# An earlier softplus for the later attention heads, a sigmoid by exponential and reciprocal, pinned splits, and decode logits by wide products and a sum

## The chip, the cores and the metric

The kernel runs on one core of a Trainium2 chip, in one launch. The metric is the device time of that launch in microseconds. A core has five engines with a queue of their own each: TensorE (PE: matrix products into PSUM, with its weight loads as PEld), VectorE (DVE), ScalarE (ACT: activation functions and casts), GpSimd (POOL) and SyncE (SP: here it only issues DMAs). An engine runs its instructions strictly in the order in which the program was laid down for it, and waits on semaphores for the others.

## The reference

One step of one layer of a decoder: 16 meta rows and 512 prompt rows go through causally, and beside them eight sequences with four new rows each read a paged cache of 512 past positions (four pages of 128). Width 2048, eight heads of 128, all in float32. Cut to what matters here:

```python
h = rmsnorm(x, g_pre)
q, k, v, ga, cb, cc, ch, gc, ma, mc = jnp.split(h @ w_in, split_offsets(), axis=-1)
a = attend(q, k, v, b_sb) * jax.nn.silu(ga)                        # 8 heads
c = cb * causal_conv(cc * ch, w_conv, b_conv) * jax.nn.silu(gc)    # width 3
merged = (jax.nn.sigmoid(ma + b_gate[:D_MODEL]) * (a @ w_pa)
          + jax.nn.sigmoid(mc + b_gate[D_MODEL:]) * (c @ w_pc))
y = x + rmsnorm(merged @ w_out, g_post)

def stick_breaking(q, k, v, q_pos, k_pos, b_sb):
    z = einsum('bqhd,bkhd->bhqk', q, k) * HEAD_DIM ** -0.5 + b_sb
    mask = k_pos[None, :] < q_pos[:, None]
    log_keep = where(mask, log_sigmoid(-z), 0.0)
    after = cumsum(log_keep, axis=3, reverse=True) - log_keep
    attn = where(mask, exp(log_sigmoid(z) + after), 0.0)
    return einsum('bhqk,bkhd->bqhd', attn, v)
```

Attention has no softmax. Each score z gives a softplus, the softplus values of the later keys are summed, and the weight is the exponential of score minus sum.

## The kernel before, in words

Every matrix product is made to float32 accuracy from three products of a cheaper kind: each operand is split into a high part (a cast on ScalarE, `act.copy`) and a low part (a subtraction on VectorE), and PE multiplies high by high, high by low and low by high. `w_split` (line 237) does this for 128 x 1024 pieces of weights, in three buffers; `split_evac` (492) for everything else. Activations lie transposed, features on the partitions and the 528 + 32 rows (560) on the free axis.

The stages follow each other on PE:

1. *Start*: load and normalise x, first products.
2. *Projections of the heads* (`head_now` 693 for heads 0 to 3, which are also attended at once; `head_later` 709 for heads 4 to 7, whose k, v and q go to DRAM scratch).
3. *Column pairs* (`pair` 987 over `seven` 949, PE's products at line 946): two times 128 columns of w_in by seven instead of eight half products. Each pair is one group of work of about 21 us, and 36 such groups follow one another: silu gates of the heads (1 to 4), the convolution (5 to 20), and the sigmoid gates MA and MC (21 to 36, the loop at 1089). The last pair of the loop is `j == 14`, `w == 1`: two blocks of columns, two halves each, so four sigmoid operations.
4. *The stage of w_pc* (1159): for each of 16 column blocks `j`, `gemm` with c (PE's line 256). Among them stand the four later heads, `HERE = {0: 4, 2: 5, 5: 6, 8: 7}`: `attend` for the head, then `gated`.
5. *The stage of w_pa* (1191), which needs all heads (a_hl), then *w_out*, then the rows' norm and the stores.

*Decode attention* is spread over stages 2 and 3 by a generator, `decode_steps` (734), which `dec_step` advances. A step of its first part is one cache page: 128 positions by four heads are multiplied with the four new rows' queries and summed over 128 elements, sixteen `tensor_tensor_reduce` operations at line 756, each with one column of `z_all` as its sum. There are 64 such pages (two halves of the heads, eight sequences, four pages). Then come decode's softplus, its sums and exponentials, and its products with the value pages (line 831), whose pool `dec3` is closed right before the pool `split0` of head 4's split parts is opened in the same place. `dec_group` (875) says how many steps each group of stage 3 takes: up to group 25 none, 2, 2, 2, then one each up to 20 and four each after that, as long as there are logits; from 26 on one each, but two at 26 and 28.

*A later head's chain* (`attend`, 599): the scores z (PE, line 610) of three groups of tiles, B, C and A; for each group softplus in four ScalarE operations (Abs, Exp, Ln, Relu: `softplus_acts`, 466), pinned to follow one another; sums and splits on VectorE and ScalarE; PE adds the sums to z (line 679); an Exp (683), a mask and a split per group; PE multiplies with v (line 689). `gated` multiplies with the silu gate (1136) and splits into `a_hl`. The next head's k, v and q are loaded (`head_loads`, 715, on SP's queue) and split (`head_split`, 1108) behind the w_pc block after the head's own, line 1174. Head 4 is loaded during the last gates and split at 1112.

What sets the order of the work: the program is laid out by a planner that goes through the traced instructions, keeps data dependences and buffers, and places each instruction on its engine when its time model says that it can begin, so an engine's order need not be the program's. `pin` (line 144, `tc.keep_in_program_order`) forbids this: a pinned instruction stays behind all that was traced before it on its engine. Before, the softplus operations of later heads and the loads of ScalarE's tables (`preload_act_table_set`) are pinned, the splits and the exponentials of attention aren't. The table that holds Exp, Ln and Abs (`LNEXP`) is loaded at 1095, after the last pair's sigmoids. `c_hl` lies in the room of `h_hi` (tag "A") and `a_hl` in that of `h_lo` (tag "B"). The c values are loaded and split at 1128 to 1132, in four buffers that the gates' loads of this stage use too.

Of the kernel before, what the change touches and what calls it, by code (L numbers as in the profile page):

```python
# [17 lines left out]
P = 128  # L18
# [42 lines left out]
def hybrid_step_kernel(  # L61
# [430 lines left out]
    def split_evac(hi, lo, raw_hi, raw_lo, scale=None):  # L492
        if scale is None:
            act.copy(hi, raw_hi)
# [53 lines left out]
    def k_split(pl, kr):  # L548
        khi = pl.tile([P, T], F32R, name="khi")
        klo = pl.tile([P, T], F32R, name="klo")  # L550
        split_evac(khi, klo, kr, kr)
        return khi, klo

    def v_split(pl, vn):
        vhi = pl.tile([P, 5, P], F32R, name="vhi", bufs=1)
        vlo = pl.tile([P, 5, P], F32R, name="vlo", bufs=1)
        split_evac(vhi[:, 0:4, :], vlo[:, 0:4, :], vn[:, 0:4, :], vn[:, 0:4, :])
        split_evac(vhi[0:16, 4, :], vlo[0:16, 4, :], vn[0:16, 4, :], vn[0:16, 4, :])
        return vhi, vlo
# [33 lines left out]
    def q_split(pl, qr):  # L593
        qhi = pl.tile([P, T], F32R, name="qhi")
        qlo = pl.tile([P, T], F32R, name="qlo")
        split_evac(qhi[:, NMETA:TP], qlo[:, NMETA:TP], qr, qr)
        return qhi, qlo

    def attend(pl, h, khi, klo, vhi, vlo, qhi, qlo, pl_a=None, after=None):
# [71 lines left out]
        for g in GROUPS:  # L671
            zt = gt[g]
            for st, c0, n, ts, m in tiles_of(g):
                ops = [(zt[:m, c0:c0 + n], neg_u[:m, :m], x) for x in sp_[st]]
                if st < 4:
                    m2, n2 = sf_[st + 1][0].shape
                    ops += [(zt[:m, c0 + n - n2:c0 + n], neg_one[:m2, :m], x) for x in sf_[st + 1]]
                for i, (o, l, x) in enumerate(ops):
                    pe.matmul(o, lhsT=l, rhs=x, start=False, stop=(i == len(ops) - 1), skip_group_check=True)  # L679
        for g in GROUPS:  # L680
            zt = gt[g]
            A = tl("e", g)
            act.activation(A, zt, AF.Exp, bias=b)
# [50 lines left out]
    def decode_steps():  # L734
# [3 lines left out]
        for said, part in (("part", units[:DEC1]), ("logits", units[DEC1:])):  # L738
            with tc.tile_pool(name="dec1", bufs=2, side="right") as d1:
                for hf, b in part:  # L740
# [8 lines left out]
                    for pg in range(NPG):  # L749
                        kt = d1.tile([P, 512], F32, name="kpage", bufs=3)  # L750
                        first(page_load(kt, kc, b, pg, cs))
                        for i, qt in enumerate(qts):
                            for t in range(2):
                                for h in range(4):
                                    junk = d1.tile([P, P], F32, name="junk", bufs=2)
                                    dve.tensor_tensor_reduce(  # L756
                                        out=junk, in0=kt[:, h * P:(h + 1) * P], in1=qt[:, t, h * P:(h + 1) * P],
                                        scale=1.0, scalar=0.0, op0=ALU.mult, op1=ALU.add,
                                        accum_out=z_all[:, pg, b, 4 * hf + h, 2 * i + t:2 * i + t + 1])
# [328 lines left out]

    for j in range(0, KD, 2):
        for w, c in ((0, COL_MA), (1, COL_MC)):  # L1090
            gs = [q_tile("g") for _ in range(2)]
            for m, half, b in pair(c + j * P, HQ):
                act.activation(gs[m][:, by_query(m, half)], b, AF.Sigmoid, bias=gate_bias(j + m, w))
            if j + 2 * w == KD:
                tc.keep_in_program_order(act.preload_act_table_set(LNEXP))
# [12 lines left out]
    def head_split(pl, x):  # L1108
        kr, vn, qr = x
        return *k_split(pl, kr), *v_split(pl, vn), *q_split(pl, qr)  # L1110

    parts = head_split(hs0, loaded)
# [10 lines left out]
    cp2 = cctx.enter_context(tc.tile_pool(name="later2", bufs=1))  # L1123
# [336 lines left out]
```

## Time and profile before

| | |
|---|---|
| median of 3 runs | 1590.72 us (1590.13 to 1592.11) |
| profiled execution | 1588.02 us |
| its span | 1586.4 us |
| mean granted clock of TensorE | 0.992 |
| ScalarE busy | 761.2 us, 48% of the span |
| GpSimd busy | 236.8 us, 15% of the span |
| weights' high parts, line 240, ScalarE | 259.4 + 132.0 us |
| weights' low parts, line 241, VectorE | 301.2 + 154.0 us |
| logits, line 756, VectorE | 1024 operations, 244.6 us by the groups' table |
| chain that ended last | 95% PE, 2% VectorE, 1% ScalarE |

The span runs from the first to the last instruction; the execution's own time is 1.6 us longer. A busy share is an average over stages with different limits, so the table of stretches, which gives each engine's busy time in a chosen part of the span, says more than the totals. The chain that ended last goes back from the last instruction: at each step to what released it, or to the instruction before it on its engine. In the list of waits a line reads: engine, what waited, what it waited for, then the total in us, how many times, and the longest. A pair of numbers in front of an instruction is its start and its length in us.

### The profile page before, as it was taken

How to read it: one execution, taken by the hardware profiler on the slowest of the kernel's cores; microseconds unless marked ns; L12 is line 12 of the kernel's file. 1: busy time of each engine (PE TensorE's matmuls, PEld its weight loads, DVE VectorE, ACT ScalarE, POOL GpSimd, SP SyncE). 2: the span in 40 equal slices, each digit the busy share in tenths (PEclk: the TensorE clock that was granted, in tenths of full speed). 3: DMA queues.
4: the chain of work that ended last, by engine and by line, in shares of the span. 5: the costliest groups of instructions: out<-in, count | busy, mean ns of one | idle time of the engine just before them, and what ended most of it. 6: DMA issues, size and time to landing. Idle time of an engine off the chain costs nothing.

```text
span 1586.4 us, 32330 instructions
## 1 busy us (share of the span) xinstructions
PE 1563.9 (99%) x12172; PEld 1528.4 (96%) x12172; DVE 1268.2 (80%) x3574; ACT 761.2 (48%) x1345; POOL 236.8 (15%) x428
## 2 busy tenths in 40 slices
PE   8999999999999999999999999999999999999997
PEld 8999999999999999999999998889899989999997
DVE  7329999956899999999999997566677667877776
ACT  6245555435444444444444467444465543355562
POOL 1133333222111011010011102321100000000000
PEclk9999999999999999999999999999999989999999
DMA  8246556344554444345456545856595525433345
GB/s 262 82 141 180 160 170 183 108 128 136 171 161 147 138 141 145 123 145 158 119 181 176 174 142 162 274 172 203 182 322 172 168 88 178 152 103 98 101 137 189
DMA packets 300675, 252.77 MB, mean 159 GB/s; under 512 B 11522, under 2 KB 268614, under 8 KB 299702
## 3 DMA queue, kind: packets, MB, share of 16 engines
q1 hardware_dynamic: 272021, 160.45, 35.1%
q0 software_dynamic: 28368, 89.98, 16.9%
q8 instruction: 95, 1.56, 0.4%
q14 instruction: 63, 0.51, 0.1%
q10 hardware_dynamic: 128, 0.27, 0.1%
HBM read 217.95 MB, written 32.71 MB: 158 GB/s over the span
## 4 chain that ended last, share of the span: by engine, by line
PE 95%; DVE 2%; ACT 1%; issue 1%; DMA 1%; DVEq 0%; ACTq 0%; SPq 0%
PE mm L946 33%; PE mm L256 27%; PE o L946 24%; PE mm L321 2%; PE z L679 1%; PE o L689 1%; PE z L321 1%; PE tp L831 1%; PE z L610 1%; PE z L1401 1%; PE tp L505 0%; PE z L1255 0%; DMA raw<-in_w_in 0%; DVE wlo L241 0%; PE tp L158 0%
## 5 line engine op out<-in xcount | busy, mean ns | idle before, releaser
L240 ACT CAST whi<-raw 128x1024 fp32r<-128x1024 f32 x247 | 259.4, 1051 | 362.2 <-PE mm L946 131.4
L241 DVE TENSOR_TENSOR wlo<-raw,whi 128x1024 fp32r<-128x1024 f32 x247 | 301.2, 1220 | 89.1 <-ACT whi L240 87.7
L946 PE MATMUL mm<-h_hi,whi 128*128 128x272 f32 (+1 forms) x1152 | 333.5, 290 | 0.7 <-ACT whi L240 0.7
L946 PE MATMUL mm<-h_hi,wlo 128*128 128x272 f32 (+1 forms) x1152 | 332.6, 290 | 0.0
L946 PE MATMUL mm<-h_lo,whi 128*128 128x272 f32 (+1 forms) x1152 | 332.5, 289 | 0.0
L946 PE MATMUL o<-t_hi,whi 128*128 128x272 f32 (+1 forms) x864 | 250.2, 290 | 1.5 <-DVE c L972 1.5
L946 PE MATMUL o<-t_lo,whi 128*128 128x272 f32 (+1 forms) x864 | 249.8, 289 | 0.0
L946 PE MATMUL o<-t_hi,wlo 128*128 128x272 f32 (+1 forms) x864 | 249.6, 289 | 0.0
L756 DVE CUSTOM_DVE_ANT_0 junk<-kpage,qb 128x128 f32<-128x128 f32 x1024 | 244.6, 284 | 4.0 <-DMA qb<-q_scr 3.6
L946 PEld LDWEIGHTS mm<-h_hi,whi 128*128 128x128 f32 x1152 | 217.3, 189 | 6.1 <-ACT whi L240 3.5
L946 PEld LDWEIGHTS mm<-h_lo,whi 128*128 128x128 f32 x1152 | 216.8, 188 | 0.9 <-issue 0.8
L946 PEld LDWEIGHTS mm<-h_hi,wlo 128*128 128x128 f32 x1152 | 216.9, 189 | 0.2
L240 ACT CAST whi<-s 128x1024 fp32r<-128x1024 f32 x126 | 132.0, 1048 | 154.6 <-PE mm L946 50.6
L241 DVE TENSOR_TENSOR wlo<-s,whi 128x1024 fp32r<-128x1024 f32 x126 | 154.0, 1222 | 62.9 <-ACT whi L240 61.4
L256 PE MATMUL mm<-h_lo,whi 128*128 128x280 f32 (+1 forms) x640 | 187.6, 293 | 0.0
L256 PE MATMUL mm<-h_hi,wlo 128*128 128x280 f32 (+1 forms) x640 | 187.1, 293 | 0.0
L256 PE MATMUL mm<-h_hi,whi 128*128 128x280 f32 (+1 forms) x640 | 186.7, 292 | 0.0
L946 PEld LDWEIGHTS o<-t_hi,whi 128*128 128x128 f32 x864 | 162.8, 188 | 2.2 <-DVE c L972 2.2
L946 PEld LDWEIGHTS o<-t_hi,wlo 128*128 128x128 f32 x864 | 163.1, 189 | 0.9 <-issue 0.8
L946 PEld LDWEIGHTS o<-t_lo,whi 128*128 128x128 f32 x864 | 163.4, 189 | 0.0
L256 PEld LDWEIGHTS mm<-h_lo,whi 128*128 128x128 f32 x640 | 120.3, 188 | 0.8
L256 PEld LDWEIGHTS mm<-h_hi,wlo 128*128 128x128 f32 x640 | 120.5, 188 | 0.5
(394 smaller groups left out, 3173.8 us busy)
## 6 DMA issues: line engine op xcount, KB each, us to landing
raw<-in_w_in SPq DMA_DIRECT2D x192, 512.0 KB, 4.5
kpage<-in_cache_k POOLq DMA_DIRECT2D x64, 256.0 KB, 3.6
qb<-q_scr POOLq DMA_DIRECT2D x32, 512.0 KB, 5.7
vpage<-in_cache_v POOLq DMA_DIRECT2D x64, 256.0 KB, 5.7
raw<-in_w_out SPq DMA_DIRECT2D x32, 512.0 KB, 4.0
gate_scr<-g POOLq DMA_DIRECT2D x32, 272.0 KB, 4.6
gt<-gate_scr POOLq DMA_DIRECT2D x16, 544.0 KB, 4.2
raw<-in_w_pc SPq DMA_DIRECT2D x16, 512.0 KB, 5.5
```

Of the source, the lines that this page charges most:

```text
L240: act.copy(hi, x)
L241: dve.tensor_sub(lo, x, hi.bitcast(F32))
L256: pe.matmul(o, lhsT=w, rhs=r[:, t0:t1], start=(k == 0 and n == 0), stop=(k == nk - 1 and n == 2))
L321: pin(pe.matmul(o, lhsT=l, rhs=r[:, k, t0:t1], start=(start and m == 0), stop=(stop and m == 2), skip_group_check=True))
L610: pe.matmul(zt[:m, c0:c0 + n], lhsT=l[:, s0:s0 + m], rhs=r[:, ts:ts + n], start=(c0 == 0 and i == 0), stop=(i == 2), skip_group_check=True)
L679: pe.matmul(o, lhsT=l, rhs=x, start=False, stop=(i == len(ops) - 1), skip_group_check=True)
L689: pe.matmul(ot[:, ts - NMETA:ts - NMETA + n], lhsT=l[:m, st, :], rhs=x[:m, c0:c0 + n], start=False, stop=(g == GROUPS[-1] and i == 2), ski ...
L756: dve.tensor_tensor_reduce(out=junk, in0=kt[:, h * P:(h + 1) * P], in1=qt[:, t, h * P:(h + 1) * P], scale=1.0, scalar=0.0, op0=ALU.mult, o ...
L831: pin(pe.matmul(po[32 * j:32 * (j + 1), :], lhsT=lhs, rhs=rhs, start=(pg == 0), stop=last and n >= len(vts) - 4, tile_position=(0, 32 * j) ...
L946: pe.matmul(o, lhsT=l[:, k, :], rhs=r, start=(start and k == 0 and m == 0), stop=(stop and k == 7 and m == 2), skip_group_check=True)
L1401: pin(pe.matmul(o, lhsT=(m1, m2)[h][:, k + 8 * (q == 1), ts], rhs=two[h][q == 2][:, :, k, :], start=(n == 0), stop=(n == 47)))
```

## The change

Five edits.

1. *The last gates.* The exponential's table is loaded ahead of the last pair, not after it, and the pair's four sigmoids are made of Exp(-x - b) on ScalarE and, on VectorE, min(e + 1, 3e38) and a reciprocal. The negated bias is one small operation (`neg_b`).
2. *The first later head.* The eight loads of c are issued in a row, and the eight splits of c become a function, `c_splits`, pinned, that `attend` calls through `first` right after head 4's softplus of group B.
3. *The next heads' parts.* `head_split` of head h+1, pinned now, is called by `attend` of head h through `between`, after the sums' products and ahead of the three exponentials, which are pinned too. Its loads come a head earlier: head 5's before the stage, then head h+2's behind head h. The pool `later2` moves to the other side of the memory.
4. *The logits.* Per page two `tensor_mul` of 128 x 1024 (the page broadcast over the rows) into a tile `kq`, and one `reduce_sum` over its last axis into `z_all`, in place of sixteen fused operations.
5. *The steps.* One step per group up to group 17, four up to 23, then the rest with two at 26.

```diff
                         kt = d1.tile([P, 512], F32, name="kpage", bufs=3)
                         first(page_load(kt, kc, b, pg, cs))
+                        kq = d1.tile([P, DT, 4, P], F32, name="kq", bufs=1)
                         for i, qt in enumerate(qts):
-                            for t in range(2):
-                                for h in range(4):
-                                    junk = d1.tile([P, P], F32, name="junk", bufs=2)
-                                    dve.tensor_tensor_reduce(
-                                        out=junk, in0=kt[:, h * P:(h + 1) * P], in1=qt[:, t, h * P:(h + 1) * P],
-                                        scale=1.0, scalar=0.0, op0=ALU.mult, op1=ALU.add,
-                                        accum_out=z_all[:, pg, b, 4 * hf + h, 2 * i + t:2 * i + t + 1])
+                            dve.tensor_mul(kq[:, 2 * i:2 * i + 2], qt.rearrange("p t (h d) -> p t h d", d=P),
+                                           kt.rearrange("p (h d) -> p h d", d=P).unsqueeze(1)
+                                           .broadcast_to([P, 2, 4, P]))
+                        dve.reduce_sum(z_all[:, pg, b, 4 * hf:4 * hf + 4, :].rearrange("p h t -> p t h"),
+                                       kq, axis=mybir.AxisListType.X)
                         yield
...
-        if n <= 25:
-            dec_step((0, 2, 2, 2)[n - 1] if n <= 4 else 1 if n <= 20 else 4, "logits")
+        if n <= 23:
+            dec_step((0, 2, 2, 2)[n - 1] if n <= 4 else 1 if n <= 17 else 4, "logits")
         else:
-            dec_step(2 if n in (26, 28) else 1)
+            dec_step(2 if n == 26 else 1)
...
+    def sigmoid_by_exp(g, x, neg_bias):
+        act.activation(g, x, AF.Exp, bias=neg_bias, scale=-1.0)
+        dve.tensor_scalar(out=g, in0=g, scalar1=1.0, scalar2=BIG, op0=ALU.add, op1=ALU.min)
+        dve.reciprocal(g, g)
...
+            last = j + 2 * w == KD
+            if last:
+                tc.keep_in_program_order(act.preload_act_table_set(LNEXP))
             for m, half, b in pair(c + j * P, HQ):
-                act.activation(gs[m][:, by_query(m, half)], b, AF.Sigmoid, bias=gate_bias(j + m, w))
-            if j + 2 * w == KD:
-                tc.keep_in_program_order(act.preload_act_table_set(LNEXP))
+                g = gs[m][:, by_query(m, half)]
+                if last:
+                    sigmoid_by_exp(g, b, neg_b[:, m:m + 1])
+                else:
+                    act.activation(g, b, AF.Sigmoid, bias=gate_bias(j + m, w))
...
-    for k in range(0, 8, 2):
-        cr = g3.tile([P, 2, TQ], F32, tag="gt", name="cr")
-        for i in range(2):
-            nc.sync.dma_start(cr[:, i, :], c_scr[k + i])
-            split_evac(c_hl[:, k + i, :], c_hl[:, 8 + k + i, :], cr[:, i, :], cr[:, i, :])
+    crs = [g3.tile([P, 2, TQ], F32, tag="gt", name="cr") for _ in range(4)]
+    for k in range(8):
+        nc.sync.dma_start(crs[k // 2][:, k % 2, :], c_scr[k])
+
+    def c_splits():
+        for k in range(8):
+            cr = crs[k // 2][:, k % 2, :]
+            split_evac(c_hl[:, k, :], c_hl[:, 8 + k, :], cr, cr, pin=pin)
...
             if after is not None:
                 softplus_acts(*elr[g], gt[g], b, pin)
+                if g == "B":
+                    first()
...
+        between()
         for g in GROUPS:
             zt = gt[g]
             A = tl("e", g)
-            act.activation(A, zt, AF.Exp, bias=b)
+            (pin if after is not None else lambda ins: ins)(act.activation(A, zt, AF.Exp, bias=b))
...
+    loaded.append(head_loads(NOW + 1, hin[1]))
     for j in range(KD):
         if j in HERE:
             h = HERE[j]
-            ot = attend(cp, h, *parts, cp2, after)
+
+            def between():
+                if h + 1 < H:
+                    parts.append(head_split(hs_[(h + 1) % 2], loaded.pop(), pin))
+
+            ot = attend(cp, h, *parts.pop(), cp2, after, between, c_splits if h == NOW else lambda: None)
             gated(h, ot, sgs.pop(h))
             sgs[h - NOW] = gate_load(h - NOW), out_load(h - NOW)
+            if h + 2 < H:
+                loaded.append(head_loads(h + 2, hin[h % 2]))
...
-        if j - 1 in HERE:
-            if h + 1 < H:
-                parts = head_split(hs_[(h + 1) % 2], head_loads(h + 1, hin[(h + 1) % 2]))
-                sgs[h + 1] = gate_load(h + 1)
+        if j - 1 in HERE and h + 1 < H:
+            sgs[h + 1] = gate_load(h + 1)
```

More of the change, by code (lines that the diff above doesn't have):

```diff
@@ L546, in outputs, with k_split, v_split @@
         pin(pool.dma_start(dst_s[0, :, :, h, :].rearrange("b t d -> (b t) d"), nat_s))
-    def k_split(pl, kr):
+    def k_split(pl, kr, pin=lambda ins: ins):
         khi = pl.tile([P, T], F32R, name="khi")
         klo = pl.tile([P, T], F32R, name="klo")
-        split_evac(khi, klo, kr, kr)
+        split_evac(khi, klo, kr, kr, pin=pin)
         return khi, klo
-    def v_split(pl, vn):
+    def v_split(pl, vn, pin=lambda ins: ins):
         vhi = pl.tile([P, 5, P], F32R, name="vhi", bufs=1)
         vlo = pl.tile([P, 5, P], F32R, name="vlo", bufs=1)
-        split_evac(vhi[:, 0:4, :], vlo[:, 0:4, :], vn[:, 0:4, :], vn[:, 0:4, :])
-        split_evac(vhi[0:16, 4, :], vlo[0:16, 4, :], vn[0:16, 4, :], vn[0:16, 4, :])
+        split_evac(vhi[:, 0:4, :], vlo[:, 0:4, :], vn[:, 0:4, :], vn[:, 0:4, :], pin=pin)
+        split_evac(vhi[0:16, 4, :], vlo[0:16, 4, :], vn[0:16, 4, :], vn[0:16, 4, :], pin=pin)
         return vhi, vlo
@@ L591, in v_proj, with q_split, attend @@
         return v_split(pl, vn)
-    def q_split(pl, qr):
+    def q_split(pl, qr, pin=lambda ins: ins):
         qhi = pl.tile([P, T], F32R, name="qhi")
         qlo = pl.tile([P, T], F32R, name="qlo")
-        split_evac(qhi[:, NMETA:TP], qlo[:, NMETA:TP], qr, qr)
+        split_evac(qhi[:, NMETA:TP], qlo[:, NMETA:TP], qr, qr, pin=pin)
         return qhi, qlo
-    def attend(pl, h, khi, klo, vhi, vlo, qhi, qlo, pl_a=None, after=None):
+    def attend(pl, h, khi, klo, vhi, vlo, qhi, qlo, pl_a=None, after=None, between=lambda: None, first=lambda: None):
         b = bsb[:, h:h + 1]
@@ L1106, in hybrid_step_kernel, with head_split @@
     hs0 = hlctx.enter_context(tc.tile_pool(name="split0", bufs=1, side="right"))
-    def head_split(pl, x):
+    def head_split(pl, x, pin=lambda ins: ins):
         kr, vn, qr = x
-        return *k_split(pl, kr), *v_split(pl, vn), *q_split(pl, qr)
-    parts = head_split(hs0, loaded)
+        return *k_split(pl, kr, pin), *v_split(pl, vn, pin), *q_split(pl, qr, pin)
+    parts, loaded = [head_split(hs0, loaded)], []
     gctx.close()
@@ L1122, in hybrid_step_kernel @@
     cp = cctx.enter_context(tc.tile_pool(name="later", bufs=1))
-    cp2 = cctx.enter_context(tc.tile_pool(name="later2", bufs=1))
+    cp2 = hlctx.enter_context(tc.tile_pool(name="later2", bufs=1, side="right"))
     ga = cctx.enter_context(tc.tile_pool(name="gated", bufs=2))
```

6 lines of the change are left out of this document (4 added, 2 removed).

## The prediction

> **What bounds the kernel now.** I read the page's head first: who is busy, and what the chain that ended last is made of.
>
> ```profile
> span 1586.4 us, 32330 instructions
> PE 1563.9 (99%) x12172; PEld 1528.4 (96%) x12172; DVE 1268.2 (80%) x3574; ACT 761.2 (48%) x1345; POOL 236.8 (15%) x428
> ```
>
> TensorE is busy for all but 22.5 us of the span, and the change neither adds nor removes a matrix product. So it can win only what PE loses, by standing idle or by running below its clock. The table of stretches says where that is (columns: PE, PEld, DVE, ACT and POOL busy, granted clock, DMA).
>
> ```profile
> 0.00:75.00 75.00, 70.03 (x509) 66.91 (x510) 41.66 (x72) 36.10 (x62) 8.99 (x21) 0.95 0.57 169
> 470.00:946.00 476.00, 475.54 (x3766) 475.12 (x3765) 457.44 (x1528) 216.49 (x318) 48.63 (x85) 1.00 0.49 147
> 946.00:1000.00 54.00, 52.27 (x397) 49.19 (x397) 40.23 (x50) 37.69 (x51) 15.72 (x26) 1.00 0.62 196
> 1000.00:1210.00 210.00, 210.00 (x1658) 194.38 (x1657) 134.07 (x183) 103.19 (x158) 35.99 (x67) 1.00 0.71 218
> 1291.00:1307.30 16.30, 12.44 (x46) 9.74 (x47) 8.54 (x21) 6.26 (x11) 0.00 (x0) 0.58 0.00 1
> 1307.30:1323.60 16.30, 16.30 (x131) 16.30 (x131) 12.66 (x26) 6.37 (x10) 1.07 (x2) 1.00 0.54 165
> 1576.00:1587.00 11.00, 0.00 (x0) 0.00 (x0) 4.91 (x11) 0.73 (x4) 0.04 (x1) 0.70 0.68 230
> ```
>
> The start loses 5.0 us and the tail 11.0; the change touches neither. Two places are left. In 946 to 1000 PE loses 1.7 us. From 1291.0 to 1307.3, where the last of the later heads holds up the stage of w_pa, PE runs 46 matmuls in 16.3 us, and the next 16.3 us hold 131. The granted clock there is 0.58. A third thing to note is that VectorE is busy 457.4 of 476 us (96%) in 470 to 946 while PE loses only 0.5 us: a second engine stands close behind the first.
>
> The chain, in order of time, shows the hole (start, length, what). The first two lines are the same steps for the head before, which has products of w_pc around it:
>
> ```profile
> 1265.67 1.44 PE z L679 x9
> 1272.49 2.39 PE o L689 x14
> ...
> 1291.39 0.55 ACT l L494
> 1291.98 0.46 PE z L679 x2
> 1292.45 2.36 PE z L679 x10
> 1295.34 0.68 ACT eA L683
> 1296.49 5.30 PE o L689 x15
> 1301.82 0.70 DVE sg L1136
> 1302.55 0.63 ACT a_hl L494
> 1303.22 4.83 PE mm L256 x22
> ```
>
> At the pace of the head before, 12 products of L679 take 12 x 1.44/9 = 1.9 us, 15 of L689 15 x 2.39/14 = 2.6 us, and the remaining 19 of the 46 take 19 x 16.3/131 = 2.4 us: 6.9 us. PE took 16.3. So this hole costs **9.4 us**, of which 16.3 - 12.4 = 3.9 is idleness and the rest half clock. With the 1.7 us at 946 and the 0.5 before it, 11.6 us is all that the change can win.
>
> **Part 1: the later heads' chain.** The four later heads run one behind another, and in the hole PE waits for the fourth. How much earlier must it be? Its z L679 would have to be handed over while products are still there to fill in: the hole runs from 1291.0 to 1303.2 with 1.9 + 2.6 = 4.5 us of work of its own, so 12.2 - 4.5 = 7.7 us earlier closes it. How head 4 starts is in ScalarE's timeline:
>
> ```profile
> 1159.23 4.47 ACT L494 CAST c_hl<-cr 128x544 fp32r<-128x544 f32 x8
> 1165.47 1.28 ACT L1095 ACT_TABLE_LOAD   x1
> 1166.77 0.61 ACT L467 ACTIVATE e<-z,bsb 128x416 f32<-128x416 f32 x1
> ...
> 1167.27 0.65 ACT L494 CAST khi<-kr 128x560 fp32r<-128x560 f32 x1
> 1171.81 0.59 ACT L467 ACTIVATE e<-z,bsb 128x416 f32<-128x416 f32 x1
> 1179.83 0.67 ACT L470 ACTIVATE rA<-z,bsb 128x512 f32<-128x512 f32 x1
> ```
>
> Pinned behind the eight casts and the table load, its twelve softplus operations run from 1166.77 to 1180.50. After the change the table comes before the last pair, group B's four operations precede the casts, and groups C and A follow the casts at 1163.70 instead of 1171.81: 8.1 us earlier. The next heads' splits, which now stand among them (khi at 1167.27 and its fellows), go behind the sums, where the queue waits for PE anyway. For the heads after it:
>
> ```profile
> ACT vhi L494 <- PE o L689: 10.7, 2, 5.6
> ACT e L467 <- PE z L610: 5.3, 1, 5.3
> ```
>
> Twice a vhi cast at the head of ScalarE's queue waits for the old head's products with the new softplus behind it. The pin removes those waits, but not all of their 10.7 us: the third head, with no vhi in the way, still waits 5.3 us for its own scores. I count 1 us per head, 2 in all. Together 8.1 + 2 = 10 us against the 7.7 needed; some goes again, because an earlier chain shares the engines with more of w_pc's work. I take 8.4 of the 9.4 us as won, with 1.0 left over. What is late next would be PE itself.
>
> The change adds waits. ScalarE's eight c_hl casts stand behind head 4's group B, which needs its scores and the table, and w_pc's first products wait for those casts. In the chain of waits the scores' first piece comes from PE at 1151.15, and ScalarE's timeline has the casts at 1159.23:
>
> ```profile
> 1151.15 0.67 PE z L610 x4
> 1158.01 0.04 PE z L610 x2
> 1161.16 1.27 PE z L610 x8
> ```
>
> Four operations of 0.6 us fit with about 5 us to spare, if PE's small remaining pieces (now spread to 1161) are run early; if they stay, the casts begin 2.4 us after 1161.2 and not at 1159.2, which makes PE wait 4.4 us. The exponentials queue behind the next head's splits and so behind its loads, issued a whole head ahead (nothing). The eight c loads and the first head_loads move up SP's queue by four issues; the planner had already placed such loads among w_pc's (nothing).
>
> **Part 2: the last gates.** Four exponentials in place of four sigmoids on ScalarE: nothing. VectorE gets four pairs of a tensor_scalar and a reciprocal, off PE's path unless they stand ahead of the c_hl subtractions. No reciprocal is in the trace; between a tensor_scalar's 0.3 us and a tensor_tensor's 0.44 (128x272) the four pairs are under 3 us, mostly beside free time. I take 0. The Trainium skill (VectorE: DVE Perf Modes, "First, the fixed hardware budget") calls Reciprocal an iterative divide with a repeat count of 8; at its 0.96 GHz eight cycles an element would be an estimated 2.3 us each, 9 us in all, of which two could stand before the casts' subtractions and cost up to 4.5 us. No run here shows it.
>
> **Part 3: the logits.** This part costs. Old, one page is 16 fused multiply-and-reduce operations. VectorE's timeline shows their pitch:
>
> ```profile
> 514.00 1.21 DVE L969 TENSOR_TENSOR raw<-raw 128x1024 f32<-128x1024 f32 x1
> 515.14 1.21 DVE L241 TENSOR_TENSOR wlo<-s,whi 128x1024 fp32r<-128x1024 f32 x1
> 516.27 0.28 DVE L756 CUSTOM_DVE_ANT_0 junk<-kpage,qb 128x128 f32<-128x128 f32 x1
> ...
> 519.31 0.28 DVE L756 CUSTOM_DVE_ANT_0 junk<-kpage,qb 128x128 f32<-128x128 f32 x1
> 519.52 0.28 DVE L756 CUSTOM_DVE_ANT_0 junk<-kpage,qb 128x128 f32<-128x128 f32 x1
> 519.73 0.28 DVE L756 CUSTOM_DVE_ANT_0 junk<-kpage,qb 128x128 f32<-128x128 f32 x1
> ```
>
> The sum of the groups' means misleads (284 ns, and 79 for the accumulator's read): they overlap, and one follows another after 0.21 us. So a page takes 16 x 0.21 = 3.4 us, not 5.8. New, a page is two products of 1024 elements, which follow each other after 1.14 us (514.00, 515.14, 516.27), and one sum of 2048. The only reductions in the trace are small:
>
> ```profile
> L1277 DVE TENSOR_REDUCE ss<-og_a x3: 164/171/202, 1566.4 to 1576.3; 128x1 f32<-128x16 f32 x2, 128x3 f32<-128x48 f32 x1
> ```
>
> 32 elements more take 31 to 38 ns more, about 1 ns an element, so 2048 make 2.2 us; at half that (the rate at which a one-source operation could go) 1.2. I take 2.2, from the reduction's own row. A page then costs 2 x 1.14 + 2.2 = 4.5 us, **1.1 us more**. At 1.2 the page would be 3.5 and this part free. The Trainium skill speaks against the change here (VectorE: DVE Perf Modes, "Rules for kernel authors"): tensor_reduce has only the 1x mode and is "the slowest DVE op". By the page's 2293 ns for 2048 such elements (its table of tiers, fp32 at 1x) a page of logits costs 4.6 us.
>
> ```profile
> 470.00:946.00 476.00, 136.60 (x1118) 1.00 0.49 147
> L756 DVE CUSTOM_DVE_ANT_0 junk<-kpage,qb x1024: 260/283/724, 122.2 to 942.4; 128x128 f32<-128x128 f32 x171
> ```
>
> L756 by stretch: 1118 instructions in 470 to 946, two per operation and 32 per page, are 35 pages, so VectorE needs 35 x 1.1 = 38 us more where 476 - 457.4 = 18.6 are free. The other 20 us must go somewhere. Either the logits finish later (now at 942.4) and use the next stretch, where VectorE is busy 134 of 210 us, or PE waits. The trace favours the first: in these 476 us the logits fill VectorE's gaps and PE loses 0.5 us. What remains is the grain: an operation of 2.2 us cannot be interrupted, where one of 0.28 stood. A split has about 3 us of lead (three buffers, 24 products of 0.126 us each), so a wait needs two long operations in a row. I take 0.1 us for half of the 64 pages: **+3 us**, between 0 and 20. The decode steps, two groups earlier in the program and perhaps 20 us later in VectorE's work, still end before head 4's splits need their room.
>
> **The sum.** -8.4 + 3 = -5.4 us on the profiled execution: 1588.02 (1.6 us around its span) to 1582.6. That execution lies 2.7 us under the median of 1590.72, so the forecast against the median is 1585.3.
>
> **The rivals.**
> *VectorE becomes the bound.* The long operations hold back the weights' low parts in 470 to 946, because logits that are behind their place in the program go first. Then the missing 20 us are paid by PE: 1590.72 - 8.4 + 20 = 1602. It decides once VectorE's need passes 476 us there, 17 more pages' worth at 1.1; 35 are due. If the four-page steps (groups 18 to 23) also crowd ahead, the whole 38 are paid: 1620. For it: 96% busy, 1.1 us a page. Against: PE's 0.5 us there.
> *The gain stays small.* The z scores' last pieces stay late, the casts' wait of 4.4 us comes, and with +3 the 9.4 shrink to 2: 1588.7.
> *The change is free.* The sum runs at 1.2 us or PE never meets a long operation: -9.4, 1581.3; with the 1.7 us at 946 gone too, 1579.6.
>
> **How the numbers follow.** Forecast 0.36 (own range 1582 to 1588), free 0.19, small gain 0.17, VectorE bound 0.28. A measurement tells apart about 0.2%, 3.2 us. Faster by more takes the forecast and the free case, less a little of the former's upper edge: 0.54; the same 0.17, slower 0.29. The range runs from 1579 (free, all of it) to 1607, past VectorE's first price of 1602; the crowded case at 1620 and what lies below 1579 are left out, together about 0.15 to 0.2.
>
> **What would show it.** Right: the stretch between w_pc's and w_pa's products has a clock near 1.0 and no wait of 1.4 us or more on a_hl; head 4's softplus has four operations before the c_hl casts; no wait of vhi on o. The new reduction reads 2.2 us and the products 1.2; logits end after 942. PE waits on wlo or c in 470 to 946 add up to some 3 us. Wrong: VectorE at 99% there with PE idle by 10 us or more, or decode values that end after 1142 and push head 4 back; on the other side, a reduction near 1.2 us.

## The result, and the profile after

The changed kernel takes 1712.68 us (1710.29 to 1714.0, 4 runs) beside 1591.41 (1590.13 to 1592.64) of the kernel before: ratio 1.0758, 95% interval 1.0742 to 1.0774, **121 us slower**. The forecast was 5 us faster. The two profiled executions, from which the readings below come, lie 126 us apart. One of the five executions of e9, 1700 us at a granted clock of 0.84, ran in a slower state of the chip and is left out of its ratio. The page's head:

```profile
span 1712.3 us, 30468 instructions
PE 1618.3 (95%) x12172; PEld 1567.0 (92%) x12172; DVE 1345.0 (79%) x1727; ACT 755.5 (44%) x1341; POOL 252.4 (15%) x428
PE 71%; DVE 18%; issue 5%; DMA 3%; ACT 2%; POOL 1%; DVEq 0%; POOLq 0%; ACTq 0%; SPq 0%
```

The third line is the chain that ended last: VectorE had 2% of it and has 18%. Where it lies is read first from PE's products by tile (first and last start): t_hi marks the column pairs, c_hl the stage of w_pc, a_hl that of w_pa. Before:

```profile
L946 PE MATMUL o<-t_hi,whi x864: 283/288/395, 372.2 to 1160.6; 128*128 128x272 f32 x135, 128*128 128x274 f32 x38
L256 PE MATMUL mm<-c_hl,whi x512: 283/288/373, 1162.3 to 1281.4; 128*128 128x272 f32 x171
L256 PE MATMUL mm<-a_hl,whi x512: 282/288/594, 1281.7 to 1393.6; 128*128 128x272 f32 x171
```

After:

```profile
L948 PE MATMUL o<-t_hi,whi x864: 282/289/576, 400.6 to 1285.7; 128*128 128x272 f32 x135, 128*128 128x274 f32 x38
L256 PE MATMUL mm<-c_hl,whi x512: 282/288/596, 1286.0 to 1414.6; 128*128 128x272 f32 x171
L256 PE MATMUL mm<-a_hl,whi x512: 283/288/428, 1414.9 to 1519.8; 128*128 128x272 f32 x171
```

400.6 - 372.2 = 28.4 us are lost ahead of the column pairs, 885.1 - 788.4 = 96.7 within them, and 233.8 - 231.3 = 2.5 in the two stages in which the heads' part was to win 8.4. Of the 28.4, 3.3 are not the logits': line 321's first product starts at 22.6 us in place of 19.3, ahead of all logits, and in e3, which has the same logits, at 19.5. The table of stretches takes the first two losses apart. Before: the stretch up to 284, the one behind it, and groups 6 to 21 of the column pairs:

```profile
75.00:284.00 209.00, 209.00 (x1603) 203.65 (x1603) 169.12 (x896) 106.34 (x216) 72.84 (x133) 1.00 0.55 165
284.00:346.00 62.00, 62.00 (x481) 60.75 (x481) 51.28 (x108) 24.49 (x50) 13.60 (x23) 1.00 0.40 120
464.20:805.20 341.00, 340.54 (x2694) 340.12 (x2693) 328.36 (x1049) 146.15 (x223) 32.45 (x57) 1.00 0.47 139
```

After, the same stretches ahead of the pairs, then groups 5 to 15, and a stretch behind the last page:

```profile
75.00:284.00 209.00, 208.08 (x1603) 203.62 (x1602) 162.55 (x194) 89.87 (x182) 72.37 (x114) 1.00 0.54 163
284.00:346.00 62.00, 48.04 (x295) 42.67 (x294) 56.54 (x79) 25.86 (x57) 19.72 (x29) 0.83 0.25 80
482.90:801.80 318.90, 272.64 (x1881) 260.79 (x1880) 318.68 (x324) 102.39 (x159) 38.94 (x66) 0.91 0.44 132
828.00:1010.00 182.00, 182.00 (x1446) 181.94 (x1445) 133.48 (x150) 84.72 (x123) 8.97 (x16) 1.00 0.39 118
```

Up to 284 PE makes its 1603 products in both; then 295 in place of 481, which is 24 us of the loss. From 482.9 to 801.8 **VectorE is busy 318.68 of 318.90 us**, and PE makes 1881 products where the old pace gives 318.9 x 2694/341 = 2519: 638 missing, 81 us at 0.127 each. Only 46 us of it are idleness. The other 35 PE loses while it is busy: the granted clock of 0.91 accounts for an estimated 25 of them (9% of 272.6), and the last 10 are not assigned. From 828 on PE loses nothing and VectorE is free for a quarter of the time. What PE waits for from 470 to 830, the two largest rows (total, times, longest):

```profile
PE o L948 <- ACT whi L240: 18.8, 12, 2.2
PE o L948 <- DVE c L974: 10.7, 10, 1.9
```

Much of it reaches PE by way of ScalarE: from 482.9 to 801.8 the casts whi in their turn wait 36 us for VectorE's sums s (lines 960, 963 and 976: 21.6, 2.5 and 12.3). VectorE's timeline shows why it is late; this is one group, from one sum of w21 and w22 (line 960) to the next:

```profile
509.63 1.23 DVE L960 TENSOR_TENSOR s<-raw 128x1024 f32<-128x1024 f32 x1
...
512.26 2.29 DVE L760 TENSOR_REDUCE z_all<-kq 128x16 f32<-128x2048 f32 x1
...
517.07 2.36 DVE L757 TENSOR_TENSOR kq<-qb,kpage 128x1024 f32<-128x1024 f32 x2
519.34 1.23 DVE L963 TENSOR_TENSOR s<-s,raw 128x1024 f32<-128x1024 f32 x1
520.48 2.29 DVE L760 TENSOR_REDUCE z_all<-kq 128x16 f32<-128x2048 f32 x1
...
524.94 2.36 DVE L757 TENSOR_TENSOR kq<-qb,kpage 128x1024 f32<-128x1024 f32 x2
...
529.48 2.29 DVE L760 TENSOR_REDUCE z_all<-kq 128x16 f32<-128x2048 f32 x1
...
533.16 2.36 DVE L757 TENSOR_TENSOR kq<-qb,kpage 128x1024 f32<-128x1024 f32 x2
...
536.56 1.23 DVE L960 TENSOR_TENSOR s<-raw 128x1024 f32<-128x1024 f32 x1
```

Three pages stand in a group, 3 x 4.5 = 13.5 us, and so it is in each of groups 4 to 16; the last sum starts at 821.5, in group 16, for which the program has asked for 42 of the 64 pages. Before, a group held one to two. Without logits a group of the kernel before needs (328.4 - 22.8 pages x 3.4)/16 = 15.7 us of VectorE: 15.7 + 13.5 = 29.2, and the eleven groups took 318.9/11 = 29.0 each, in place of 21.3.

The new operations themselves, by groups (busy, mean ns):

```profile
L757 DVE TENSOR_TENSOR kq<-qb,kpage 128x1024 f32<-128x1024 f32 x128 | 151.7, 1226 | 3.2 <-DMA qb<-q_scr 3.1
L760 DVE TENSOR_REDUCE z_all<-kq 128x16 f32<-128x2048 f32 x64 | 146.3, 2286 | 0.0
L1098 DVE RECIPROCAL g<-g 128x272 f32<-128x272 f32 x4 | 7.4, 1841 | 0.0
```

The sums by their own line, with first and last start:

```profile
L760 DVE TENSOR_REDUCE z_all<-kq x64: 2217/2283/2326, 131.0 to 821.5; 128x16 f32<-128x2048 f32 x64
```

The sum is the 2.2 us forecast (and the 2293 ns that the Trainium skill, VectorE: DVE Perf Modes, "The perf-mode tier table", gives for 2048 fp32 elements in the 1x mode). The reciprocal is not: 1.84 us.

### The profile page after: what moved, and what is told of

The parts are those of the page before. It is cut to its first block, busy times and chain, and to the rows that moved or that the text cites. A ratio compares the mean times of both kernels' runs of the same rounds, so it can differ in the third digit from the quotient of the medians.

```text
span 1712.3 us, 30468 instructions
## 1 busy us (share of the span) xinstructions
PE 1618.3 (95%) x12172; PEld 1567.0 (92%) x12172; DVE 1345.0 (79%) x1727; ACT 755.5 (44%) x1341; POOL 252.4 (15%) x428
## 4 chain that ended last, share of the span: by engine, by line
PE 71%; DVE 18%; issue 5%; DMA 3%; ACT 2%; POOL 1%; DVEq 0%; POOLq 0%; ACTq 0%; SPq 0%
PE mm L256 23%; PE mm L948 21%; PE o L948 16%; DVE kq L757 5%; DVE wlo L241 4%; DVE z_all L760 2%; DMA raw<-in_w_in 2%; PE mm L321 2%; PE z L681 1%; PE z L321 1%; PE o L692 1%; PE tp L833 1%; PE z L610 1%; DVE raw L971 1%; DMA qb<-q_scr 1%
## 5 line engine op out<-in xcount | busy, mean ns | idle before, releaser
L948 PE MATMUL o<-t_hi,whi 128*128 128x272 f32 (+1 forms) x864 | 261.4, 302 | 33.2 <-ACT whi L240 20.2
L948 PE MATMUL o<-t_hi,wlo 128*128 128x272 f32 (+1 forms) x864 | 261.1, 302 | 5.8 <-DVE wlo L241 5.8
L948 PEld LDWEIGHTS mm<-h_hi,whi 128*128 128x128 f32 x1152 | 220.2, 191 | 19.1 <-ACT whi L240 15.8
L948 PEld LDWEIGHTS mm<-h_hi,wlo 128*128 128x128 f32 x1152 | 219.3, 191 | 8.6 <-DVE wlo L241 8.3
L948 PEld LDWEIGHTS mm<-h_lo,whi 128*128 128x128 f32 x1152 | 219.8, 191 | 0.1
L948 PEld LDWEIGHTS o<-t_hi,whi 128*128 128x128 f32 x864 | 172.1, 199 | 38.8 <-ACT whi L240 23.0
L948 PEld LDWEIGHTS o<-t_hi,wlo 128*128 128x128 f32 x864 | 172.6, 200 | 8.9 <-DVE wlo L241 8.6
L948 PEld LDWEIGHTS o<-t_lo,whi 128*128 128x128 f32 x864 | 172.3, 199 | 0.5 <-issue 0.4
L757 DVE TENSOR_TENSOR kq<-qb,kpage 128x1024 f32<-128x1024 f32 x128 | 151.7, 1226 | 3.2 <-DMA qb<-q_scr 3.1
L760 DVE TENSOR_REDUCE z_all<-kq 128x16 f32<-128x2048 f32 x64 | 146.3, 2286 | 0.0
L256 PEld LDWEIGHTS mm<-h_hi,whi 128*128 128x128 f32 x640 | 121.6, 190 | 1.0 <-ACT raw L565 0.6
```

Of the source, the lines that this page charges most:

```text
L256: pe.matmul(o, lhsT=w, rhs=r[:, t0:t1], start=(k == 0 and n == 0), stop=(k == nk - 1 and n == 2))
L757: dve.tensor_mul(kq[:, 2 * i:2 * i + 2], qt.rearrange("p t (h d) -> p t h d", d=P), kt.rearrange("p (h d) -> p h d", d=P).unsqueeze(1) .br ...
L760: dve.reduce_sum(z_all[:, pg, b, 4 * hf:4 * hf + 4, :].rearrange("p h t -> p t h"), kq, axis=mybir.AxisListType.X)
L948: pe.matmul(o, lhsT=l[:, k, :], rhs=r, start=(start and k == 0 and m == 0), stop=(stop and k == 7 and m == 2), skip_group_check=True)
```

## The experiments

Theory "order": the planner puts the new pages where VectorE has no room, and PE pays for the crowd. Theory "cost": the loss follows VectorE's added work, wherever it stands. For the heads, the theories stand with each run. The first runs take the change apart.

**e1, the change without its logits** (line 756's old loop and the old steps in the changed kernel):

```diff
-                            dve.tensor_mul(kq[:, 2 * i:2 * i + 2], ...
-                        dve.reduce_sum(z_all[:, pg, b, 4 * hf:4 * hf + 4, :] ...
+                            for t in range(2):
+                                for h in range(4):
+                                    dve.tensor_tensor_reduce(out=junk, ...
```

> The change without its logits: the heads' and the gates' part, with the old sixteen operations a page and the old steps. In the changed kernel the time from the first product of c to the last of a_hl is 233.8 us against 231.3, so the hole at the end of w_pc's stage is closed but about as much is lost at its front, where PE waits and the reciprocals take 1.84 us each. Theory 'paid back at the front': 1589 to 1594 us beside 1591. Theory of the prediction (8.4 us won, the reciprocals hidden): 1583. Theory 'the chain got worse': 1600 or more.

Measured 1593.83 us beside 1590.72: ratio 1.0016 (1.0006 to 1.0027). Paid back, as the first theory had it; why is told with e5 to e8.

**e3, the logits alone** in the kernel before, with the old steps; of the change only this:

```diff
-                                    dve.tensor_tensor_reduce(out=junk, ...
+                            dve.tensor_mul(kq[:, 2 * i:2 * i + 2], ...
+                        dve.reduce_sum(z_all[:, pg, b, 4 * hf:4 * hf + 4, :] ...
```

> The logits' part alone in the kernel before, with the old steps. Theories 'order' and 'cost' both put nearly the whole 121 us here: 1710 to 1716, with three pages in each of the groups 4 to 16. If the two parts add up otherwise (the heads' part holding some of the loss), under 1700.

Measured 1712.14: ratio 1.0757 (1.0741 to 1.0774). The logits' part is the whole loss. The new steps play no part: the planner's layout has the same three pages a group with the old ones.

**e4, the logits pinned**:

```diff
-                            dve.tensor_mul(kq[:, 2 * i:2 * i + 2], ...)
+                            pin(dve.tensor_mul(kq[:, 2 * i:2 * i + 2], ...))
-                        dve.reduce_sum(z_all[...], kq, ...)
+                        pin(dve.reduce_sum(z_all[...], kq, ...))
...
+        if n <= 29:
+            dec_step((0, 2, 2, 2)[n - 1] if n <= 4 else 1 if n <= 20 else 2, "logits")
+        else:
+            dec_step(2)
```

> As e3, but every wide product and sum is pinned to its place in the program, and the steps are one page a group up to group 20 and two from 21 to 29. The work on VectorE is the same as in e3. Theory 'order' (PE loses because the planner crowds three pages, 13.8 us of VectorE, into groups that have 5.4 us free): a conv group then needs 15.8 + 4.6 = 20.4 us of VectorE in 21.2 and loses nothing, a gates group 13.3 + 9.2 = 22.5 and loses 1.3, nine of them 12; with the 28 us that are lost before the column pairs about 40 over the kernel before: 1631. Theory 'cost' (the loss goes with the added VectorE time, wherever it stands): 1700 or more.

Measured 1674.93: ratio 1.0529 (1.0513 to 1.0545), 84 us slower, between the two. The same operations in another order save 37 us, which "cost" alone denies; but a loss of 40 was the forecast, and less than a third of the loss went away. The table of stretches of e4, groups 7 to 10 (one page each) and 23 to 28 (two each):

```profile
524.00:613.00 89.00, 86.34 (x675) 85.27 (x674) 81.15 (x92) 36.67 (x57) 6.84 (x12) 1.00 0.43 125
885.00:1031.00 146.00, 134.08 (x1020) 129.22 (x1019) 134.06 (x115) 60.64 (x85) 16.68 (x29) 1.00 0.49 149
```

VectorE is at 91 and 92%, not at its limit, and PE still makes 675 of 703 and 1020 of 1153 products (at 2694 in 341 us). That loss is 1 us a group with one page and 3 with two, where the lack of room alone gives 0 and 1.3. That a long operation in a fixed place makes a split late is the likely reason, but it is argued and not shown: in the second stretch VectorE itself waits 7.0 us for casts whi and 4.9 for loads of weights. Ahead of the column pairs e4 loses 18.7 us (they start at 390.9), not the 28 of its expectation. Besides, decode's value products end at 1244.0, behind the first product of c at 1238.8, and the stages of w_pc and w_pa take 241.1 us in place of 231.3.

**e10, products without sums**, which leaves the logits' sums out (z_all is zero):

```diff
+    dve.memset(z_all, 0.0)
...
-                        dve.reduce_sum(z_all[:, pg, b, 4 * hf:4 * hf + 4, :] ...
```

> e3 without the sums: z_all is set to zero once and the logits' sums are left out, so a page is 2.3 us of VectorE and not 3.4 as in the kernel before; everything behind it runs as ever. Laid out, the planner places five to six such pages in each of groups 4 to 9. Theory 'cost': less VectorE work than before, so no loss, 1590 or less. Theory 'order': six pages are 13.7 us again beside 15.8 of a conv group, 29.5 in 21.2; six groups lose 8 us each: 1640.

Measured 1640.42: ratio 1.031 (1.0289 to 1.0332). VectorE has a third less work for a page than in the kernel before, and the kernel is 49 us slower. As the whole explanation "cost" falls. The stretch of groups 4 to 9 in e10:

```profile
429.70:602.60 172.90, 146.38 (x1011) 139.85 (x1010) 168.59 (x181) 56.03 (x84) 36.41 (x61) 0.92 0.62 188
```

VectorE is busy 98% there; 5 to 6.5 pages stand in each group, 28.8 us long.

What rule the planner follows can be guessed from layouts alone, which were not run: with the changed kernel's sum issued twice, three and four times per page, it places 2, 1.5 and 1.2 pages in a group. If a sum counts as two products, the groups hold 3 x 4, 2 x 6, 1.5 x 8 and 1.2 x 10 product-times, and e10 five to six and a half pages of 2: about **12** each time. At the 1.14 us at which products follow each other that is 13.7 us, where 21.3 - 15.7 = 5.6 are free. So it seems to fill what its own prices leave, and by its prices a group has more than twice the room that it has on the chip. The old page stood 22.8/16 = 1.43 times in a group; if the same 12 limited it, it was priced at 8.4 products, 9.6 us, where it takes 3.4, and the old order was good because two wrong prices met. That is an inference: its prices are in no trace, and the old pages stood unevenly, 1.1 to 2 in a group. The pages' places are what the traces show.

**e9, wide logits beside the heads' projections only** (the first 24 pages):

```diff
+                        if said == "part":
+                            (two products and a sum)
+                        else:
                             (the sixteen operations)
```

> The kernel before with wide products and sums for the first 24 pages only, which lie beside the projections of the heads; the other 40 keep the sixteen operations. In e4 the first column pair came 29 us later than in the kernel before, and only the wide operations among the heads lie ahead of it. Theory 'order' puts 28 to 30 us of the loss there and the rest into the column pairs: 1620. If the loss at that place came from what follows (loads of the second part, queue of GpSimd): 1591.

Measured ratio 1.0184 (1.0163 to 1.0206), 29 us, with runs from 1612.1 to 1622.1, so 20 to 30 us: a loss that these 24 pages make by themselves. That e4 was 29 us late here is a wrong figure in the expectation: it was 18.7, and the changed kernel 28.4. In the changed kernel the loss falls between 284 and 346, where head 3's sums, the last pages and the tsum stage's sums (line 920) want VectorE at once (56.5 of 62 us). PE's largest waits there:

```profile
PE z L681 <- ACT l L494: 5.0, 2, 2.8
PE z L681 <- DVE e L495: 2.9, 2, 2.0
```

The runs do not show that order alone makes this loss. The same 24 pages stand here in every version, and the loss follows their work: at 2.3 us a page (e10) the first pair starts 1.9 us later than before, at 4.5 us 26.6 later in e3 and, pinned, 18.7 in e4. So order has some 8 us of it at least, and "cost" fits the rest as well; what e10 refutes is "cost" within the column pairs.

**The heads' and gates' part.** e2 is e1 with the old sigmoids, and the table behind them:

```diff
...
-                if last:
-                    sigmoid_by_exp(g, b, neg_b[:, m:m + 1])
-                else:
-                    act.activation(g, b, AF.Sigmoid, bias=gate_bias(j + m, w))
+                act.activation(gs[m][:, by_query(m, half)], b, AF.Sigmoid, bias=gate_bias(j + m, w))
+            if j + 2 * w == KD:
+                tc.keep_in_program_order(act.preload_act_table_set(LNEXP))
```

> As e1, with the last gates' sigmoids as before and the table loaded after them. If the four reciprocals (8.5 us of VectorE with their additions) are what is lost at the front, this is 3 to 6 us faster than e1, about 1586. If the eight c casts behind group B's softplus are what is lost, they come even later here, behind the table too: 3 to 8 us slower than e1.

Measured 1593.75: ratio 1.0019 (1.0009 to 1.003), as slow as e1: neither forecast. What the reciprocals cost is replaced by PE's one wait of 4.8 us for the c casts, behind group B's softplus and the table. e11 is the gates' part alone, these lines the other way round in the kernel before:

> The gates' part alone: the last pair's sigmoid by exponential and reciprocal, the table ahead of it; heads, splits and logits as before. VectorE was saturated from 1160 to 1190 in every run with it (29.1 to 29.7 us of 30; 27.3 before), and PE lost 4 to 9 us there. Theory 'the reciprocals are paid at the front': 2 to 5 us slower than before, 1593 to 1596. Theory of the prediction (they are hidden): the same, or faster where head 4's softplus starts earlier, 1587 to 1591.

Measured 1592.06: ratio 1.0006 (0.9994 to 1.0018), not to be told from no change. Yet PE loses at the front. Two stretches of the kernel before:

```profile
1160.00:1190.00 30.00, 30.00 (x238) 29.84 (x237) 27.27 (x51) 22.66 (x38) 3.24 (x6) 1.00 1.01 318
1280.00:1310.00 30.00, 26.13 (x150) 22.95 (x149) 20.58 (x47) 13.63 (x24) 1.09 (x2) 0.77 0.29 88
```

The same of e11:

```profile
1160.00:1190.00 30.00, 26.40 (x198) 26.01 (x197) 28.80 (x49) 21.42 (x38) 2.17 (x4) 0.94 0.83 272
1280.00:1310.00 30.00, 26.69 (x182) 24.41 (x182) 20.78 (x45) 16.25 (x29) 2.17 (x4) 0.92 0.32 111
```

40 products, 5 us, are missing at the front, and 32 more are made where the hole was. A loss at the front costs little: the heads' chain sets the end of w_pc's stage, and work of PE that comes late fills the hole that waits for the chain.

e5, e6 and e7 each undo one edit of e1, e8 all three:

```diff
# e5
-            (pin if after is not None else lambda ins: ins)(act.activation(A, zt, AF.Exp, bias=b))
+            act.activation(A, zt, AF.Exp, bias=b)
# e6
-            ot = attend(cp, h, *parts.pop(), cp2, after, between, ...
+            ot = attend(cp, h, *parts.pop(), cp2, after, lambda: None, ...
...
         if j - 1 in HERE and h + 1 < H:
+            parts.append(head_split(hs_[(h + 1) % 2], loaded.pop(0)))
# e7
-    ... c_splits if h == NOW else lambda: None)
+    c_splits()   (ahead of the loop, not pinned)
```

> e1 with the three exponentials of a later head not pinned. In e1 a pinned exponential stands behind the cast of the group before, so the three start at 1270.12, 1272.11 and 1273.77 (3.65 us from first to last) where the kernel before has 1.42. Theory 'the pins stretch the chain': 2.2 us less per head, of which the hole at the end gets most: 3 to 6 us faster than e1, 1588 to 1591. Theory 'only the front counts': within 1 us of e1.

> e1 with the next head's splits back behind the w_pc block after the head's own, not pinned; loads stay early. In e1 they land amid the softplus of the head before (khi at 1248.29 ahead of eA's exponential at 1251.48) and their low parts cost VectorE 2.3 us there, but no vhi cast waits for o any more. Theory 'the splits stretch the chain': 2 us or more faster than e1. Theory of the prediction (they save 1 us per head or more): 2 to 5 us slower than e1.

> e1 with the c splits ahead of head 4's softplus again, not pinned. In e1 PE makes 194 products between 1160 and 1190 where the kernel before makes 242, 6 us, and waits for c_hl and for gt. Theory 'the front pays': those 6 us come back; head 4's softplus begins up to 4.5 us later, and if the chain sets the end the hole grows by as much: between 1588 and 1593. If the reciprocals are what is paid at the front, as slow as e1.

> All three undone together: what is left of the heads' and gates' part are the table and sigmoid by exponential, and the loads a head earlier. If each of the three edits costs, this is the fastest of the four, 1584 to 1588, since head 4's softplus still needs no table load behind the casts. If one of them is what wins, this is no faster than e1 with the other two undone, and at about 1591.

| run | us | ratio (95%) | head 4 starts | to head 5 | to 6 | to 7 | to a_hl | chain |
|---|---|---|---|---|---|---|---|---|
| before | 1590.7 to 1591.8 | | 1166.8 | 39.3 | 36.2 | 32.7 | 27.5 | 135.8 |
| e1 | 1593.83 | 1.0016 (1.0006, 1.0027) | 1162.4 | 43.3 | 36.5 | 36.2 | 30.1 | 146.1 |
| e2 | 1593.75 | 1.0019 (1.0009, 1.003) | 1167.5 | 35.6 | 35.8 | 37.1 | 32.4 | 141.0 |
| e5 | 1592.84 | 1.0019 (1.0008, 1.0029) | 1160.0 | 44.7 | 37.0 | 34.8 | 29.6 | 146.1 |
| e6 | 1593.58 | 1.0018 (1.0007, 1.0029) | 1160.5 | 48.0 | 35.9 | 33.1 | 31.8 | 148.9 |
| e7 | 1589.69 | 0.9996 (0.9987, 1.0005) | 1165.8 | 39.4 | 35.0 | 37.1 | 28.5 | 140.0 |
| e8 | 1592.25 | 1.0009 (1.0, 1.0018) | 1164.4 | 45.1 | 33.8 | 35.4 | 27.0 | 141.3 |
| e11 | 1592.06 | 1.0006 (0.9994, 1.0018) | 1166.7 | 45.4 | 33.8 | 35.4 | 26.5 | 141.1 |
| e12 | 1589.19 | 0.9985 (0.9973, 0.9997) | 1169.2 | 37.3 | 37.0 | 34.8 | 27.0 | 136.2 |

The starts are those of the first Abs of each head's softplus (line 467) in ScalarE's timeline, and the end is the start of the last a_hl cast; each is from the one execution that was profiled. An earlier start of head 4 is worth nothing: in e1 it is 4.4 us earlier and head 5 only 0.4. With the reciprocals the first head takes 43 to 48 us (e7 alone 39.4), without them 36 to 39. e5 and e6 gain nothing over e1 that can be measured: both theories of stretched chains miss, and so does the prediction's for e6, by which e6 would have been 2 to 5 us slower. Only e7, with the c splits ahead of the softplus again, is faster than e1 beyond the intervals, by 3 us as the ratios have it; e8's interval overlaps e1's, so the three edits' costs don't add up. What makes e7's first head the shortest of those with reciprocals stays open.

**e12**: sigmoids as before, c splits first, next head's splits between sums and exponentials, exponentials not pinned (the edits of e2, e5 and e7 in e1).

> The kernel before with only what has not been shown to cost: sigmoids as before, c splits first, the loads a head early and the next head's splits pinned between sums and exponentials, the exponentials not pinned. If the front's loss comes from the reciprocals and the c casts' place, the front is as before, and the hole shrinks by the 3 us that it shrank by in the other variants: 1587 to 1589. If the hole is set by the heads' own period of 36 us whatever stands around: 1591.

Measured 1589.19 beside 1591.77: 2.4 us faster by the ratio, the only version that beats both kernels. The interval (0.9973 to 0.9997) is just clear of no change, and as one of twelve versions it could be so by chance. Its trace has the front as before (239 products from 1160 to 1190, before 238), as the expectation had it, but the hole has not shrunk (148 products from 1280 to 1310, before 150): where the 2.4 us would come from is not shown.

## Why the prediction was wrong, point by point

**The step that failed: "The trace favours the first: in these 476 us the logits fill VectorE's gaps and PE loses 0.5 us", and with it +3 us.** The operation's price was right: 4.5 us a page, the sum 2.29 us. But the gap-filling was taken for a property of the logits; it was a property of the planner's layout of the old operation. The new one it lays out at 13.5 us of logits in groups with 5.6 free, and PE loses 96.7 us in the column pairs in place of the 3. e10 has less work than the old kernel in a crowded layout and loses 49; e4 has the new work in a looser layout and loses 84 in place of 121. How the 84 divide between the added work, the long operations and the front stays open.

**The rival "VectorE becomes the bound"** (0.28) was the right mechanism: VectorE at its limit holds back what PE needs. Its reason, "logits that are behind their place in the program go first", was the wrong way round, for they ran ahead of it, all 64 pages where 42 were asked for. Its prices of 20 and 38 us counted only the 1.1 us added per page, but a crowded page costs all its time: the 40 pages' room in groups 17 to 28, where VectorE then stands free, is lost as well. To that comes the clock, a term that the sum lacked here, though the hole of 9.4 us (3.9 idle) had shown it: of 81 us in groups 5 to 15 idleness is 46 and the clock an estimated 25. And about 25 us fell ahead of the pairs, where I counted nothing: 169 of 209 us of VectorE until 284 look roomy, and the stretch behind it, in which three claims meet, was not looked at by itself.

**Heads, "8.1 us earlier" plus "1 us per head".** In e1 head 4's first group starts 4.4 us earlier; groups C and A, for which the 8.1 was counted, start only 2.5 and 1.0 us earlier (1169.28 and 1173.08 in place of 1171.81 and 1174.06), and nothing was won. That the next heads' splits "go behind the sums" failed: ScalarE's timeline of e1 shows them amid head 6's softplus:

```profile
1246.70 0.68 ACT L467 ACTIVATE eA<-z,bsb 128x512 f32<-128x512 f32 x1
...
1247.78 0.60 ACT L672 COPY o<-zero_c 128x512 f32<-128x512 f32 x1
1248.29 0.67 ACT L494 CAST khi<-kr 128x560 fp32r<-128x560 f32 x1
1248.85 0.81 ACT L494 CAST vhi<-vn 128x512 fp32r<-128x512 f32 x2
1249.57 0.61 ACT L494 CAST qhi<-qr 128x512 fp32r<-128x512 f32 x1
...
1251.48 0.62 ACT L468 ACTIVATE eA<-eA 128x512 f32<-128x512 f32 x1
...
1270.12 0.61 ACT L686 ACTIVATE e<-z,bsb 128x416 f32<-128x416 f32 x1 [3.00 <-PE z L681]
1271.23 0.54 ACT L494 CAST hi<-e 128x416 fp32r<-128x416 f32 x1 [0.51 <-DVE e L624]
1272.11 0.61 ACT L686 ACTIVATE e<-z,bsb 128x416 f32<-128x416 f32 x1 [0.33 <-PE z L681]
1273.33 0.54 ACT L494 CAST hi<-e 128x416 fp32r<-128x416 f32 x1 [0.62 <-DVE e L624]
1273.77 0.68 ACT L686 ACTIVATE eA<-z,bsb 128x512 f32<-128x512 f32 x1
```

So, against what the section on the kernel says, a pin does not hold an instruction behind all that was traced before it. The trace fits a pin that reaches one instruction back: khi is pinned behind the clearing of o (line 672), which is not pinned itself and stands ahead. And each exponential, pinned behind the cast of the group before, waits for that group's mask: 3.65 us from first to last. The waits of vhi on o are gone, as forecast; e5 shows that freeing the exponentials wins nothing measurable on top.

**"I take 0" for the reciprocals** was wrong in size: four at 1.84 us plus the additions are 8.5 us, against "under 3". The Trainium skill's iterative divide (VectorE: DVE Perf Modes, "First, the fixed hardware budget") gave an estimated 2.3 us each, which is much nearer. The price of that was right all the same, by luck: e11 is within 0.2%, because the heads' chain and not PE sets the stage's end. **The c casts' wait** that was priced at 4.4 us for the small pieces, "if they stay", is there in part (2.3 us on c_hl in e1, 4.8 in e2).

## What to carry to other kernels

Where a planner lays out the program, an operation that is replaced changes not only its own time but the place that the planner gives it and what stands around it: count how many of them it places per unit of the bound engine's work, in the layout, before costing them one by one. An engine at 96% beside a bound engine at 100% had no room for a worse order, and TensorE's idleness is not the whole bill: here 46 us of it went with 81 us of lost products. An earlier start of a chain was worth nothing here, where the stage's other work on the chain's engines moved into the time that it freed.

## What the runs showed of the hardware

A reciprocal of 128 x 272 takes 1.84 us on VectorE, 6.8 ns an element, where a tensor_scalar of that shape takes 0.3. Sixteen fused multiply-and-sums of 128 elements (3.4 us) beat two products and one sum of the same data (4.5 us). The granted clock can be below 1 with short idle times alone: in groups 5 to 15 PE waits 46 us of 319, never more than 2.4 at a time, at a clock of 0.91, and loses 35 us more while busy. In e4, from 885 to 1031, it waits 11.9 us of 146, at most 0.8 at a time, at 1.00.
